# Gate and up tiles of a feed-forward by Strassen's seven products

## The chip, the cores and the metric

The kernel runs on one core of one Trainium2 chip. The metric is the device time of one execution in microseconds, the median of several runs. Five engines matter: TensorE (matrix products, in the profile PE, its weight loads PEld), VectorE (DVE), ScalarE (ACT), GpSimd (POOL) and SyncE (SP, which issues the transfers).

## The reference

A trunk of two layers for 128 prompt tokens and 512 latent tokens, 640 together, 1024 channels wide, all in float32. Each layer normalizes, projects, runs three mixers (a gated convolution, attention, a bidirectional state-space scan), merges them, and then adds a feed-forward:

```
h = rms_norm(x, norm2_g) * (1 + scale2) + shift2
x = x + gate2 * ((silu(h @ w_ffn_gate) * (h @ w_ffn_up)) @ w_ffn_down)
```

The gate and up matrices are 1024 x 2816 and the down matrix 2816 x 1024. shift2, scale2 and gate2 come from a modulation product of a condition vector with `w_ada`. The two groups of tokens share the weights and differ in the conditions.

## The kernel before

**Numbers.** A product of float32 is made of three products of float32r: each operand is split exactly into a high and a low part, and high x high, high x low and low x high are added up in PSUM. A product of 128 channels in, 128 channels out and 640 tokens is therefore three products times two halves of 320 tokens (HN), six matmuls of 128x128 weights against 320 columns (`gemm`, line 732). Activations are kept channels on partitions, as pairs of tiles (high, low) of 640 columns.

**Weights.** They come as a stream of blocks in the order of use (`order`, from line 283): a block of up to 1024 words per partition, 512 KB, is loaded by SyncE into one of three `wr` buffers (`w_load`, line 365). The `converter` (line 376) makes it a `wh` tile of a high part (a cast on ScalarE) and a low part (a subtraction on VectorE). There are three `wh` buffers (line 178), and a block may be converted when it is at most two ahead of the one that the products took last. `w_get` (line 393) hands a converted block to the products. Modulation blocks are in the same stream; they are used unsplit, in products of 32 condition rows (`ada_step`, line 545).

**Order of the work.** The order on each engine is fixed when the program is written out. The main products are a generator. Before each group of six matmuls it tells what they need, and `pump` (line 431) then emits those pieces of side work that can start earlier by a clock of estimated times. The converter is side work of the first priority. The estimates (`Clock`, `Engine`, from line 58) cost a matmul 133 ns for 320 columns, a VectorE instruction 70 ns and 1.04 ns a column, a ScalarE instruction 100 ns and 0.83 ns a column. Each engine then runs its list in order and waits on semaphores.

**The feed-forward** (line 1742 on) follows the second normalization (`norm`, line 660), which makes the eight pairs of h. It has two halves of 11 tiles of 128 hidden channels. For each tile the gate product (48 matmuls) and the up product (48) go to a PSUM tile each; `ev_g` makes tanh and a gated value, `ev_u` multiplies and splits the result into the hidden pair. After 11 tiles follow the eight tiles of the down product over those 11 blocks (66 matmuls each), added to x by `gated` (line 751), three VectorE instructions. In layer 0 one modulation block follows nearly each gate tile. The first pair of a feed-forward runs both tiles side by side (`pair_gemm`), since h is still being made.

After the second half's gate and up tiles of layer 0, `ssm_begin` starts the state-space side work of layer 1, which prepares its matrices under the second down product and the first stages of layer 1. The gate that reads its results (`glu`) comes after the query projections.

**Buffers.** PSUM has four tiles of two banks (`gps`). `c2` tiles of 640 columns: 57. `pt` tiles of 1280 columns (line 176): four, which attention uses, and the state-space side work; the feed-forward of before doesn't.

All instructions are recorded at one helper's line (L130), so the profile is read by tiles and shapes: `wh<-wr` is a conversion, `bps<-c,wh` a main product, `c<-bps` an evacuation, `bps<-wr,csT` a modulation product.

## Time and profile before

| | us |
|---|---|
| median of 3 runs | 2639.64 |
| lowest and highest | 2638.81, 2642.4 |
| span of the profiled execution | 2643.2 |
| TensorE busy | 2554.0 |
| VectorE busy | 1580.0 |
| ScalarE busy | 1016.2 |
| GpSimd busy | 0.2 |

The profiled execution has no other time of its own on record than its span, which is 3.6 us over the median of the runs and 0.8 over the highest. Busy times of matmuls overlap one another, so a busy TensorE says that it has no gap and not how quick it is; that is read from the number of matmuls in a stretch. A wait is put down to the instruction whose signal came last.

### The profile page before, as it was taken

How to read it: one execution, taken by the hardware profiler on the slowest of the kernel's cores; microseconds unless marked ns; L12 is line 12 of the kernel's file. 1: busy time of each engine (PE TensorE's matmuls, PEld its weight loads, DVE VectorE, ACT ScalarE, POOL GpSimd, SP SyncE). 2: the span in 40 equal slices, each digit the busy share in tenths (PEclk: the TensorE clock that was granted, in tenths of full speed). 3: DMA queues.
4: the chain of work that ended last, by engine and by line, in shares of the span. 5: the costliest groups of instructions: out<-in, count | busy, mean ns of one | idle time of the engine just before them, and what ended most of it. 6: DMA issues, size and time to landing. Idle time of an engine off the chain costs nothing. (4 is left out here: it accounts for less than half of the span.)

```text
span 2643.2 us, 44920 instructions
## 1 busy us (share of the span) xinstructions
PE 2554.0 (97%) x18683; PEld 2460.0 (93%) x18683; DVE 1580.0 (60%) x2982; ACT 1016.2 (38%) x1835; POOL 0.2 (0%) x4
## 2 busy tenths in 40 slices
PE   6999999999899999999989999999998999999998
PEld 4899999999888999999989999989998989999998
DVE  5888887788744433233677897578776453333333
ACT  4334336566622421122253333466664242212222
POOL 0000000000000000000000000000000000000000
PEclk8999999999999999999989999999999999999999
DMA  9433321121057233333334233212211633223222
GB/s 266 133 110 110 110 76 54 60 69 41 9 168 215 75 110 88 88 112 105 89 119 113 66 112 102 74 51 69 59 41 56 206 113 88 62 75 88 72 63 73
DMA packets 404411, 250.53 MB, mean 95 GB/s; under 512 B 57768, under 2 KB 392432, under 8 KB 404208
## 3 DMA queue, kind: packets, MB, share of 16 engines
q1 hardware_dynamic: 404208, 247.66, 31.9%
q8 instruction: 147, 2.41, 0.4%
q14 instruction: 56, 0.46, 0.1%
HBM read 227.49 MB, written 20.12 MB: 94 GB/s over the span
## 5 line engine op out<-in xcount | busy, mean ns | idle before, releaser
L130 PE MATMUL bps<-c,wh 128*128 128x320 f32 x12672 | 1952.1, 312 | 37.9 <-ACT c L130 18.4
L130 PEld LDWEIGHTS bps<-c,wh 128*128 128x128 f32 x12672 | 1876.4, 189 | 75.9 <-issue 25.1
L130 DVE TENSOR_TENSOR wh<-wr,wh 128x1024 fp32r<-128x1024 f32 (+2 forms) x308 | 353.8, 1153 | 223.6 <-ACT wh L130 213.8
L130 DVE TENSOR_TENSOR c<-c,c 128x512 f32<-128x512 f32 (+10 forms) x722 | 407.5, 590 | 71.6 <-ACT c L130 62.1
L130 ACT CAST wh<-wr 128x1024 fp32r<-128x1024 f32 (+2 forms) x308 | 303.7, 990 | 318.1 <-PE bps L130 177.9
L130 DVE SCALAR_TENSOR_TENSOR c<-c,bps 128x640 f32<-128x640 f32 (+1 forms) x108 | 83.2, 771 | 245.9 <-ACT c L130 169.6
L130 ACT CAST c<-c 128x640 fp32r<-128x640 f32 (+3 forms) x172 | 102.3, 621 | 327.0 <-DVE c L130 322.4
L130 DVE TENSOR_TENSOR c<-c,bps 128x640 f32<-128x640 f32 (+1 forms) x108 | 82.8, 769 | 205.9 <-PE bps L130 202.6
L130 PE MATMUL bps<-wh,c 128*128 128x256 f32 x1440 | 181.0, 284 | 2.0 <-ACT c L130 1.8
L130 ACT ACTIVATE c<-bps 128x640 f32<-128x640 f32 (+1 forms) x108 | 71.7, 664 | 285.3 <-PE bps L130 274.7
L130 PE MATMUL bps<-ident,c 128*128 128x128 f32 (+1 forms) x1115 | 159.1, 280 | 19.6 <-DVE c L130 7.4
L130 PEld LDWEIGHTS bps<-wh,c 128*128 128x128 f32 x1440 | 175.4, 191 | 2.7 <-ACT c L130 2.2
L130 PE MATMUL bps<-c,c 128*128 128x320 f32 (+2 forms) x960 | 159.5, 297 | 8.3 <-ACT c L130 4.5
L130 PEld LDWEIGHTS bps<-ident,c 128*128 128x128 f32 (+1 forms) x1115 | 132.6, 145 | 30.2 <-issue 8.9
L130 PEld LDWEIGHTS bps<-c,c 128*128 128x128 f32 x960 | 134.3, 191 | 13.4 <-ACT c L130 9.6
L130 ACT COPY c<-bps 64x256 f32<-64x256 f32 (+7 forms) x210 | 85.5, 445 | 155.8 <-PE bps L130 154.3
L130 ACT ACTIVATE c<-c 128x640 f32<-128x640 f32 (+4 forms) x93 | 65.3, 716 | 206.7 <-DVE c L130 206.5
L130 ACT ACTIVATE c<-bps,mx 128x640 f32<-128x640 f32 (+1 forms) x160 | 113.3, 713 | 36.1 <-DVE mx L130 35.6
L130 DVE TENSOR_REDUCE mx<-bps 128x1 f32<-128x640 f32 (+1 forms) x136 | 109.6, 809 | 26.4 <-PE bps L130 26.1
L130 DVE TENSOR_TENSOR pt<-bps,pt 128x640 fp32r<-128x640 f32 (+1 forms) x136 | 109.1, 810 | 15.3 <-ACT pt L130 14.5
L130 ACT CAST pt<-bps 128x640 fp32r<-128x640 f32 (+1 forms) x136 | 92.3, 687 | 26.6 <-PE bps L130 25.7
L130 PE MATMUL bps<-pt,c 128*128 128x256 f32 (+1 forms) x656 | 96.0, 292 | 2.9 <-DVE pt L130 2.1
(98 smaller groups left out, 1072.7 us busy)
## 6 DMA issues: line engine op xcount, KB each, us to landing
wr<-in_w_in_dram SPq DMA_DIRECT2D x104, 512.0 KB
wr<-in_w_ada_dram SPq DMA_DIRECT2D x62, 512.0 KB
wr<-in_w_ffn_gate_dram SPq DMA_DIRECT2D x44, 512.0 KB
wr<-in_w_ffn_up_dram SPq DMA_DIRECT2D x44, 512.0 KB
c<-in_w_ada_dram SPq DMA_DIRECT2D x68, 256.0 KB
wr<-in_w_ffn_down_dram SPq DMA_DIRECT2D x32, 384.0 KB
wr<-in_w_ffn_down_dram SPq DMA_DIRECT2D x32, 320.0 KB
wr<-in_w_proj_attn_dram SPq DMA_DIRECT2D x16, 512.0 KB
```

What stands on the lines that cost most here:

```text
L130: res = f(*args, **kw)
```

## The change

From the fourth tile of hidden channels on (PLAIN = 3), the gate tile and the up tile of the same 128 channels become one 2x2 product: the columns of the matrix on the left are gate and up, its rows the first and the last 512 input channels, and the right operand's columns are the two halves of 320 tokens. Of the eight products of quarters, 12 matmuls each (four blocks of channels, three float32r products), Strassen's scheme (in the form with shared sums) needs seven.

- **Sums of activations** (`sums`, once a layer, as side work): from the unsplit h, which `norm` now keeps (`plain`), four combinations of quarters for each of the four pairs of channel blocks, split again.
- **Sums of weights** (`pair_units`): a pair of tiles comes as two blocks, ra (upper rows of gate and up) and rb (lower rows). Three combinations on VectorE give four units: (ra, difference), (two sums), (rb plain), (one sum alone). The high and low parts of the first, second and fourth are made as before. For the third, ScalarE writes the high part of rb and, with scale -1, minus the high part (the write rounds to float32r), and a transfer issued by GpSimd with `accum_op=add` adds rb to the latter in place. `rb` and the sums live in `pt` tiles.
- **Products** (`glu_pair`): the seven quarter products go to the four banks of two PSUM tiles X and Y, with additions of first results in tiles z and e. `quarters` (not shown) cuts h and its sums into the right operands. The rest of the evacuation is side work (`tail`).
- **Four parts**: tiles 0 to 3, then 4 to 9, 10 to 15 and 16 to 21, each followed by its share of the down products (4 or 6 blocks). So x is added to four times.
- The normalization makes its channel blocks in the order KS = 0, 4, 1, 5, ..., and the first pair takes them in that order.
- In layer 0 the modulation blocks are put behind the pairs, as many as before.

The diff, cut to its core (in the rest comments are dropped and arguments passed on):

```diff
@@ -44,8 +44,9 @@
 WR = 3
 NTILES = 57
 RES = 1
-FF_HALF = KF // 2
-FD_ROWS = (((0, 6), (6, 5)), ((11, 6), (17, 5)))
+FF_PARTS = ((0, 4), (4, 6), (10, 6), (16, 6))
+PLAIN = 3
+KS = (0, 4, 1, 5, 2, 6, 3, 7)
 GQ = 4
 GE = GQ * NCH
...
+    def wpair(key, src1, src2, c0):
+        for h in range(2):
+            order.append((key + (h,), [src[512 * h:512 * h + 512, c0:c0 + 128] for src in (src1, src2)], 4, 128))
+        units.extend(key + (j,) for j in range(4))
...
         for m in range(8):
             tblk(("o", l, m), a["w_out"][l], 0, KD, 128 * m, 128)
         ada_gap(GN)
-        for half in range(2):
-            for m in range(FF_HALF * half, FF_HALF * half + FF_HALF):
-                tblk(("fg", l, m), a["w_ffn_gate"][l], 0, KD, 128 * m, 128)
-                tblk(("fu", l, m), a["w_ffn_up"][l], 0, KD, 128 * m, 128)
+        for r0, nr in FF_PARTS:
+            for m in range(r0, r0 + nr):
+                if m < PLAIN:
+                    tblk(("fg", l, m), a["w_ffn_gate"][l], 0, KD, 128 * m, 128)
+                    tblk(("fu", l, m), a["w_ffn_up"][l], 0, KD, 128 * m, 128)
+                else:
+                    wpair(("fgu", l, m), a["w_ffn_gate"][l], a["w_ffn_up"][l], 128 * m)
+                    ada_blk(ada_n(("fgu", l, m)))
             for m in range(KD):
-                for r0, nr in FD_ROWS[half]:
-                    wblk(("fd", l, m, r0), a["w_ffn_down"][l], r0, nr, 128 * m, 128)
+                wblk(("fd", l, m, r0), a["w_ffn_down"][l], r0, nr, 128 * m, 128)
         ada_gap(GF)
     assert not ada_o
...
-        key, src, nr, ncol = order[i]
-        t = wrp.tile([128, 1024], F32, tag="wr", name="wr")
-        clk.ring("wr", t.name, WR)
-        sp.dma_start(t[:, :nr * ncol].rearrange("p (k m) -> p k m", k=nr), src.rearrange("(k p) m -> p k m", p=128))
+        key, srcs, nr, ncol = order[i]
+        if key[0] == "fgu" and key[3]:
+            t = f32(ptp.tile([128, 2, TK], F32R, tag="pt", name="pt").rearrange("p a b -> p (a b)"))
+        else:
+            t = wrp.tile([128, 1024], F32, tag="wr", name="wr")
+            clk.ring("wr", t.name, WR)
+        n = nr * ncol
+        for j, src in enumerate(srcs):
+            sp.dma_start(t[:, n * j:n * j + n].rearrange("p (k m) -> p k m", k=nr), src.rearrange("(k p) m -> p k m", p=128))
         wraw[i] = t
         wst["load"] += 1
...
     def converter():
-        for i, (key, src, nr, ncol) in enumerate(order):
-            yield lambda: i in wraw and i < wst["use"] + 2 - wst["pair"]
+        u = 0
+        pair = []
+        for i, (key, srcs, nr, ncol) in enumerate(order):
+            def may():
+                return i in wraw and u < wst["use"] + 2 - wst["pair"]
+            yield may
             if key[0] == "ada":
-                wtile[i] = wraw.pop(i)[:, :nr * ncol].rearrange("p (k m) -> p k m", k=nr)
+                wtile[u] = wraw.pop(i)[:, :nr * ncol].rearrange("p (k m) -> p k m", k=nr)
+                u += 1
+                continue
+            n = nr * ncol
+            if key[0] == "fgu":
+                pair.append(wraw.pop(i))
+                if key[3]:
+                    for hl in pair_units(pair, lambda: u < wst["use"] + 2 - wst["pair"]):
+                        if hl is None or callable(hl) or isinstance(hl, tuple):
+                            yield hl
+                            continue
+                        wtile[u] = hl[0]
+                        u += 1
+                    pair = []
                 continue
             yield wraw[i], "act", "wh"
             t = wraw.pop(i)
-            hl = whp.tile([128, 2, 1024], F32R, tag="wh", name="wh")
-            clk.ring("wh", hl.name, 3)
-            n = nr * ncol
+            hl = wh_tile()
             act.copy(hl[:, 0, :n], t[:, :n])
             yield hl, "dve"
             sub(hl[:, 1, :n], t[:, :n], f32(hl[:, 0, :n]))
-            wtile[i] = [hl[:, r, :n].rearrange("p (k m) -> p k m", k=nr) for r in range(2)]
+            wtile[u] = [hl[:, r, :n].rearrange("p (k m) -> p k m", k=nr) for r in range(2)]
+            u += 1
             w_load()
+    def pair_units(pair, may):
+        ra, rb = pair
+        q = lambda t, j: t[:, 512 * j:512 * j + 512]
+        def unit(hl, n):
+            return [[hl[:, r, :n].rearrange("p (j k m) -> p j k m", k=4, m=128) for r in range(2)]]
+        def both(t, n):
+            hl = wh_tile()
+            act.copy(hl[:, 0, :n], t[:, :n])
+            yield hl, "dve"
+            sub(hl[:, 1, :n], t[:, :n], f32(hl[:, 0, :n]))
+            yield unit(hl, n)
+        yield ra, rb, "dve"
+        sm_ = f32(ptp.tile([128, 2, TK], F32R, tag="pt", name="pt").rearrange("p a b -> p (a b)"))
+        stt(q(sm_, 0), q(ra, 1), -1.0, q(rb, 1), OP.mult, OP.subtract)
+        sub(q(ra, 1), q(ra, 0), q(ra, 1))
+        yield ra, "act", "wh"
+        yield from both(ra, 1024)
+        yield may
+        yield sm_, "dve"
+        stt(q(sm_, 1), q(sm_, 0), -1.0, q(ra, 0), OP.mult, OP.subtract)
+        w_load()
+        yield sm_, "act", "wh"
+        yield from both(sm_, 1024)
+        yield may
+        yield rb, "act", "wh"
+        hl = wh_tile()
+        act.copy(hl[:, 0], rb[:, :1024])
+        act.activation(hl[:, 1], rb[:, :1024], AF.Copy, scale=-1.0)
+        pool.dma_start(f32(hl[:, 1]), rb[:, :1024], accum_op=OP.add)
+        yield unit(hl, 1024)
+        yield may
+        yield rb, sm_, "dve"
+        sub(q(sm_, 0), q(rb, 0), q(sm_, 1))
+        w_load()
+        yield sm_, "act", "wh"
+        yield from both(sm_, 512)
...
+    def quarter(ps, b, w, i, xs, first):
+        K = len(xs)
+        for k, x in enumerate(xs):
+            yield (w[0],) + x + (() if k else (ps,))
+            for n, (r, s) in enumerate(((0, 0), (0, 1), (1, 0))):
+                mm(ps[:, b, 0:HN], w[r][:, i, k, :], x[s], first and k == 0 and n == 0, k == K - 1 and n == 2)
+    def sums(ts_, hs, out):
+        pend = []
+        for j in range(4):
+            a, b = v2(ts_[j]), v2(ts_[j + 4])
+            yield ts_[j], ts_[j + 4], "dve"
+            t1, t2 = c2(), c2()
+            sub(t1[:, 0:HN], a[:, 0], a[:, 1])
+            sub(t1[:, HN:], b[:, 1], a[:, 1])
+            add(t2[:, 0:HN], b[:, 1], t1[:, 0:HN])
+            sub(t2[:, HN:], b[:, 0], t2[:, 0:HN])
+            ts_[j] = ts_[j + 4] = None
+            r = []
+            for t in (t1, t2):
+                hi, lo = c2(F32R), c2(F32R)
+                act.copy(hi, t)
+                yield hi, "dve"
+                sub(lo, t, f32(hi))
+                r.append((hi, lo))
+            out.append(r)
...
+    def glu_pair(l, m, x, hid):
+        X, Y = gps(), gps()
+        z = c2()
+        w = w_get(("fgu", l, m, 0))
+        yield from quarter(X, 0, w, 0, x["b11"], True)
+        act.copy(z[:, 0:HN], X[:, 0, 0:HN])
+        yield from quarter(Y, 1, w, 1, x["t3"], True)
+        act.copy(z[:, HN:], Y[:, 1, 0:HN])
+        w = w_get(("fgu", l, m, 1))
+        yield from quarter(Y, 0, w, 0, x["t1"], True)
+        add(z[:, HN:], z[:, HN:], Y[:, 0, 0:HN])
+        yield from quarter(X, 1, w, 1, x["t2"], True)
+        w_ahead(2)
+        e = f32(ptp.tile([128, 2, TK], F32R, tag="pt", name="pt").rearrange("p a b -> p (a b)"))
+        add(z[:, 0:HN], z[:, 0:HN], X[:, 1, 0:HN])
+        add(e[:, 2 * HN:3 * HN], z[:, 0:HN], z[:, HN:])
+        w = w_get(("fgu", l, m, 2))
+        yield from quarter(X, 0, w, 0, x["b21"], False)
+        s = c2()
+        act.activation(s[:, 0:HN], X[:, 0, 0:HN], AF.Tanh, scale=0.5)
+        stt(s[:, 0:HN], s[:, 0:HN], 1.0, X[:, 0, 0:HN], OP.add, OP.mult)
+        release(X)
+        yield from quarter(Y, 1, w, 1, x["t4"], False)
+        w = w_get(("fgu", l, m, 3))
+        yield from quarter(Y, 0, w, 0, x["b22"], False)
+        add(v2(e[:, 0:TK]), pv2(Y), z[:, None, 0:HN].to_broadcast([128, 2, HN]))
+        release(Y)
+        act.activation(s[:, HN:], e[:, 0:HN], AF.Tanh, scale=0.5)
+        def tail():
+            yield s, "dve"
+            stt(s[:, HN:], s[:, HN:], 1.0, e[:, 0:HN], OP.add, OP.mult)
+            mul(s, s, e[:, HN:3 * HN])
+            hi, lo = c2(F32R), c2(F32R)
+            act.copy(hi, s)
+            yield hi, "dve"
+            sub(lo, s, f32(hi))
+            hid.append((hi, lo))
+        side = Side(tail(), -0.4)
+        for _ in range(ada_n(("fgu", l, m))):
+            yield from ada_step()
+        return side
...
             if m == 6:
                 ada_flush()
         stat.append(pend.pop(0))
-        hs = yield from norm(stat, xs, s2T[l], modT[l][:, 3], FILL2)
+        hp = [None] * KD
+        hs = yield from norm(stat, xs, s2T[l], modT[l][:, 3], FILL2, KS, hp)
+        tt_ = []
+        side = Side(sums(hp, hs, tt_), -0.3)
         ssm = None
-        for half in range(2):
+        for part, (m0, nm) in enumerate(FF_PARTS):
             hid = []
-            for m in range(FF_HALF * half, FF_HALF * half + FF_HALF):
+            tails = []
+            for m in range(m0, m0 + nm):
+                if m >= PLAIN:
+                    if not side.done:
+                        pump(until=side)
+                    tails.append((yield from glu_pair(l, m, quarters(hs, tt_), hid)))
+                    continue
                 s = c2()
                 def ev_g(ps):
@@ -1755,23 +1937,26 @@
                     hid.append(split(s))
                 if m == 0:
-                    yield from pair_gemm(("fg", l, m), ("fu", l, m), hs, ev_g, ev_u)
+                    yield from pair_gemm(("fg", l, m), ("fu", l, m), hs, ev_g, ev_u, KS)
                     continue
                 yield from tile_gemm(("fg", l, m), hs, ev_g)
                 yield from tile_gemm(("fu", l, m), hs, ev_u)
-            if not half:
+            for x in tails:
+                if not x.done:
+                    pump(until=x)
+            final = m0 + nm == KF
+            if not final:
                 ada_flush(l, 5)
             else:
                 ada_flush()
                 stat = []
+                hs = tt_ = None
                 ssm = ssm_begin(l + 1) if l + 1 < DEPTH else None
             for m in range(KD):
                 ps = gps()
-                for r0, nr in FD_ROWS[half]:
-                    w = w_get(("fd", l, m, r0))
-                    r1 = r0 - FF_HALF * half
-                    yield from gemm(ps, w, 0, hid[r1:r1 + nr], r1 == 0, r1 + nr == FF_HALF)
-                if half:
+                w = w_get(("fd", l, m, m0))
+                yield from gemm(ps, w, 0, hid)
+                if final:
                     clk.calm = m >= KD - 2 and l + 1 < DEPTH
                     if l + 1 < DEPTH and m >= 8 - GF:
```

## Rows read from the trace of the kernel before

**Rows 1.** The page: busy times of the engines, and TensorE's granted clock in 40 slices

```profile
PE 2554.0 (97%) x18683; PEld 2460.0 (93%) x18683; DVE 1580.0 (60%) x2982; ACT 1016.2 (38%) x1835; POOL 0.2 (0%) x4
...
PEclk8999999999999999999989999999999999999999
```

**Rows 2.** Stretches: length, then busy PE, PEld, DVE, ACT, POOL; clock; DMA share; GB/s

```profile
860.84:902.50 41.66, 41.66 (x282) 40.33 (x283) 21.91 (x25) 20.22 (x30) 0.00 (x0) 1.00 0.25 74
1024.00:1101.50 77.50, 77.50 (x531) 77.50 (x530) 22.59 (x38) 13.68 (x17) 0.00 (x0) 1.00 0.27 79
1276.90:1354.50 77.60, 72.01 (x523) 70.15 (x521) 69.63 (x212) 23.96 (x48) 0.00 (x0) 1.00 0.32 85
...
2380.00:2540.00 160.00, 160.00 (x1093) 160.00 (x1092) 55.49 (x60) 36.85 (x44) 0.00 (x0) 1.00 0.26 75
```

**Rows 3.** Timeline of weight loads (layer 0) and evacuations (layer 1): start, length, instructions

```profile
1001.44 0.16 PEld L130 LDWEIGHTS bps<-wr,csT 128*32 128x32 f32 x8 [0.19 <-issue]
1002.01 14.08 PEld L130 LDWEIGHTS bps<-c,wh 128*128 128x128 f32 x96 [0.41 <-issue]
1016.28 0.16 PEld L130 LDWEIGHTS bps<-wr,csT 128*32 128x32 f32 x8 [0.19 <-issue]
...
2182.82 0.70 ACT L130 ACTIVATE c<-bps 128x640 f32<-128x640 f32 x1 [2.77 <-PE bps L130]
...
2196.90 0.70 ACT L130 ACTIVATE c<-bps 128x640 f32<-128x640 f32 x1 [4.50 <-PE bps L130]
```

**Rows 4.** Timeline of VectorE in the first down product of layer 0

```profile
1053.23 1.13 DVE L130 SCALAR_TENSOR_TENSOR c<-bps,g2T,c 128x128 f32<-128x128 f32 x3 [2.82 <-PE bps L130]
...
1062.91 1.14 DVE L130 SCALAR_TENSOR_TENSOR c<-bps,g2T,c 128x128 f32<-128x128 f32 x3 [2.82 <-PE bps L130]
```

**Rows 5.** Groups by shape, VectorE, then ScalarE: count, busy us, mean ns, idle before

```profile
L130 DVE TENSOR_TENSOR wh<-wr,wh 128x1024 fp32r<-128x1024 f32 x244 | 297.5, 1222 | 141.0 <-ACT wh L130 131.3
L130 DVE TENSOR_TENSOR c<-c,c 128x640 fp32r<-128x640 f32 x116 | 93.2, 824 | 58.4 <-ACT c L130 58.3
L130 DVE TENSOR_TENSOR c<-c,c 128x512 f32<-128x512 f32 x136 | 91.7, 688 | 2.9
L130 DVE TENSOR_TENSOR c<-c,bps 128x640 f32<-128x640 f32 x92 | 75.0, 819 | 203.1 <-PE bps L130 202.6
L130 DVE TENSOR_TENSOR c<-c,bps 128x320 f32<-128x320 f32 x16 | 7.7, 482 | 2.8 <-ACT c L130 2.8
...
L130 ACT CAST wh<-wr 128x1024 fp32r<-128x1024 f32 x244 | 254.5, 1046 | 196.0 <-DMA wr<-in_w_proj_attn_dram 78.8 <-PE bps L130 77.0 <-DMA wr<-in_w_out_dram 32.5
L130 ACT CAST c<-c 128x640 fp32r<-128x640 f32 x116 | 81.8, 727 | 327.0 <-DVE c L130 322.4 <-issue 3.6
L130 ACT CAST c<-bps 128x512 fp32r<-128x512 f32 x32 | 19.0, 594 | 0.0
L130 ACT ACTIVATE c<-c 128x320 f32<-128x320 f32 x16 | 7.6, 474 | 15.7 <-DVE c L130 15.7
L130 ACT ACTIVATE c<-bps 128x320 f32<-128x320 f32 x16 | 7.0, 436 | 23.0 <-PE bps L130 15.7 <-issue 7.3
```

**Rows 6.** Timeline: issues of weight loads by SyncE, and the casts that waited for them

```profile
2101.62 0.37 SPq L130 DMA_DIRECT2D wr<-in_w_out_dram  x1
...
2107.82 0.37 SPq L130 DMA_DIRECT2D wr<-in_w_out_dram  x1
...
2105.49 1.05 ACT L130 CAST wh<-wr 128x1024 fp32r<-128x1024 f32 x1 [2.54 <-DMA wr<-in_w_out_dram]
...
2112.85 1.05 ACT L130 CAST wh<-wr 128x1024 fp32r<-128x1024 f32 x1 [2.11 <-DMA wr<-in_w_out_dram]
```

**Rows 7.** DMA queues, 1359.5 to 1366 (the spill): packets, MB, share of 16 engines

```profile
q1 hardware_dynamic: 989, 2.11, 86.3%
```

**Rows 8.** DMA queues, 2380 to 2530 (layer 1's feed-forward, weight loads)

```profile
q1 hardware_dynamic: 22728, 11.45, 26.1%
```

**Rows 9.** Timeline of SyncE: the last store of state-space outputs, and their gate's weights

```profile
1657.45 0.34 SPq L130 DMA_DIRECT2D yd<-c  x1
...
1694.76 12.77 SPq L130 DMA_DIRECT2D wr<-in_w_glu_dram  x2
```

More of the change, by code (lines that the diff above doesn't have):

```diff
@@ L389, in converter, with w_ahead @@
             sub(hl[:, 1, :n], t[:, :n], f32(hl[:, 0, :n]))
[L390 removed]
+            wtile[u] = [hl[:, r, :n].rearrange("p (k m) -> p k m", k=nr) for r in range(2)]
+            u += 1
             w_load()
+    def pair_units(pair, may):
[34 more added lines that the diff above has]
+        yield from both(sm_, 512)
     def w_get(key):
[L394 to L395 removed]
+        u = wst["use"]
+        assert units[u] == key, (units[u], key)
         wst["use"] += 1
[L397 removed]
+        while u not in wtile:
             cvt.step()
[L399 removed]
+        return wtile.pop(u)
+    def w_ahead(n):
+        while wst["use"] + n - 1 not in wtile and wst["use"] + n - 1 < len(units):
+            cvt.step()
     sides = []
@@ L664, in norm @@
         clk.calm = False
-        hs = []
+        hs = [None] * KD
         def low(k):
@@ L669, in low @@
             sub(lo, h, f32(hi))
-        ts_ = []
-        for k in range(KD):
+            if plain is None:
+                ts_[k] = None
+        ts_ = [None] * KD if plain is None else plain
+        last = None
+        for n, k in enumerate(ks):
             yield ps, "dve"
             t = c2()
-            ts_.append(t)
+            ts_[k] = t
             mul(v2(t), v2(xs[k]), pv2(ps))
-            if k == KD - 1:
+            if n == KD - 1:
                 release(ps)
-            if k:
-                low(k - 1)
-            hs.append((c2(F32R), c2(F32R)))
+            if n:
+                low(last)
+            last = k
+            hs[k] = (c2(F32R), c2(F32R))
             act.activation(t[:, :TP], t[:, :TP], AF.Identity, bias=sh[:, k, 0:1], scale=sc[:, k, 0:1])
@@ L684, in norm @@
             act.copy(hs[k][0], t)
-        low(KD - 1)
+        low(last)
         return hs
@@ L729, in reload_x, with gemm @@
         return xs
-    def gemm(ps, w, c0, acts, first=True, last=True):
+    def gemm(ps, w, c0, acts, first=True, last=True, ks=None):
         K = len(acts)
-        for k in range(K):
+        for i, k in enumerate(ks or range(K)):
             x = acts[k]
-            if last and k >= K - RES:
+            if last and i >= K - RES:
                 clk.spare = 1
-            yield (w[0],) + x + (() if k else (ps,))
+            yield (w[0],) + x + (() if i else (ps,))
             for n, (r, s) in enumerate(((0, 0), (0, 1), (1, 0))):
```

31 lines of the change are left out of this document (20 added, 11 removed).

## Prediction

> **What bounds the kernel now.** The page's busy times come first [rows 1]: TensorE is busy 97% of the span, VectorE 60%, ScalarE 38%, GpSimd not at all, and TensorE's granted clock stands at the upper level, 2.4 GHz, but for dips. Then a table of stretches [rows 2]: in the down products of layer 0 and in half of layer 1's feed-forward TensorE has no idle time (77.50 of 77.50 us, 160.00 of 160.00), with VectorE at a third. So the feed-forward costs what its matmuls cost. The last gives 160.00 / 1093 = 146 ns for one. The timeline gives it exactly [rows 3]: 96 weight loads, one for each matmul of a gate and an up tile, take 14.08 us, 146.7 ns each. A pair of tiles takes 14.08 us in layer 1 (two evacuations one after the other start at 2182.82 and 2196.90) and 14.84 in layer 0, where each is followed by one modulation block of 0.76 us. A down tile of 11 blocks, 66 matmuls, takes 9.68 us [rows 4], the same rate.
>
> **What goes.** 19 of the 22 pairs of each layer need 7 x 4 x 3 = 84 matmuls instead of 96. 19 x 12 x 0.1467 = 33.4 us per layer, 66.9 in all, if TensorE stays without waits; a pair then takes 12.32 us (13.08 with its modulation block). The down products keep their number.
>
> **What TensorE has to wait for now.** A pair takes four units of converted weights, of 24, 24, 24 and 12 matmuls: 3.52, 3.52, 3.52 and 1.76 us; they start at 0, 3.52, 7.04 and 10.56. There are three wh buffers, so the third unit (rb, the plain quarters) gets the buffer of the fourth unit of the pair before, free at 0, and must be there at 7.04. What stands between:
>
> 1. VectorE adds 640 columns from PSUM, 0.82, and ScalarE takes the tanh of 320, 0.47 [rows 5]; both are issued ahead of the unit's casts and ScalarE runs in order.
> 2. ScalarE casts 1024 columns, 1.05, and copies them negated (no row has this; the cast's 1.05). With steps of about 0.06 between engines that is 3.4 us after the last matmul.
> 3. In layer 1 the copy of the first product stands in front too: by the planner's costs the tanh ends 1.30 us after the pair, and the last point of the first quarter at which side work is emitted is at 1.20 (9 matmuls of 133 ns). That product is done at 1.76, its copy takes 0.44 to 0.47, so the casts end at 4.3. In layer 0 the modulation block puts the planner's TensorE 1.1 us later, and the casts go first.
> 4. GpSimd's accumulating transfer, 512 KB. Call it L, from the end of the negated copy to its landing.
>
> Behind it lie units three and four, 5.28 us. So a pair takes 3.4 + L + 5.28 = 8.7 + L in layer 0 (the modulation block lies inside), 9.6 + L in layer 1, and no less than 13.08 and 12.32.
>
> **What L is.** The trace has no transfer issued by GpSimd, and none that adds. A plain load of 512 KB lands 3.87 and 5.03 us after its issue (2101.62 to 2105.49, 2107.82 to 2112.85), the second behind modulation loads [rows 6]. Loads in 512-byte packets move 11.45 MB in 26.1% of 16 engines' 150 us, 18.3 GB/s for an engine, 293 for all [rows 8]: 1.79 us for a block, which leaves 2.1 us fixed. Long rows (the residual's spill, 2560 bytes each) move 2.11 MB in 86.3% of 6.5 us, 376 GB/s [rows 7]: 1.4 us for one pass over 512 KB. An accumulation has to read both operands. If the reads overlap fully, L is 2.1 + 1.4 = 3.5; if they follow one another, 4.9; with three passes behind a whole weight block 2.1 + 4.2 + 1.8 = 8.1. Below, no issue can be cheaper than a load's without its fixed part: 1.4. I take 4.2, between one pass and two; the nearest row is the 3.87 of the load.
>
> A rule of the Trainium skill bears on this, "DMA: Bandwidth & Descriptors", the section on the anatomy of one DMA on the gpsimd path: about 2.0 us fixed and the bytes over 436 GB/s, that is 3.2 us for this size, by which the sum below would end at 2599. It is stated for plain copies; our load's 2.1 fixed agrees, its rate doesn't (293 GB/s). No run here shows a GpSimd transfer yet.
>
> With 4.2, layer 0 needs 12.9 and stays at 13.08: 19 x 1.76 = 33.4 us gained. Layer 1 takes 13.8: 19 x 0.28 = 5.3 us gained. Together 38.7 of the 66.9.
>
> **VectorE and ScalarE in a pair** [rows 5]. VectorE: four combinations of 512 columns (4 x 0.69), low parts of 1024, 1024 and 512 (2.44 + 0.69), five instructions on 320 (5 x 0.48), three on 640 (3 x 0.82): 10.8 us, where it had 4.9. It fits in 12.3 with little to spare. ScalarE: four of 1024 columns, 0.6, four of 320 and one of 640, 7.3 us. The order matters more: the e tile comes from a ring of four which it shares with rb and sm, and takes the place of rb. So the add into e waits on VectorE until the transfer has landed, and behind it stand two combinations (1.38), then the cast (1.05) and the low part (1.22) of the next pair's first unit, with a 0.48 between: e 0.48 and these give 4.6 plus some 0.3 of steps, 4.9 us after the landing, against TensorE's 5.28. It holds by 0.4 us.
>
> **Smaller terms.**
> - Ends of parts, four in a layer instead of two. From the last matmul to the last hidden half: 0.82 + 0.47 + 0.48 + 0.82 + 0.73 + 0.82 and steps, 4.4 us; the first down tile's other blocks cover 5 x 0.88 = 4.4 (parts of six) or 2.6 (part of four), and down weights' low parts (0.95) run on VectorE between. Before, 10 blocks covered 2.4 us of it. I take 4 a layer, 8 together; bounds 0 and 16.
> - Starts of parts, three a layer: combinations, cast and low part 3.7 us, with the gated sums (1.30) between 4.9, against a last down tile of 5.28 or 3.52: 3 together, bounds 0 and 8.
> - The sums of activations: 16 halves at 0.48 and 8 low parts at 0.82, 14.3 us of VectorE. The three plain pairs have 41.66 - 21.91 = 19.8 us free [rows 2]. I take 1; if the first paired tile needs that time as well, up to 5.
> - The second down stretch of layer 0 covers the state-space preparation of layer 1. It was 8 x 9.68 = 77 us and becomes 8 x 5.28 = 42. VectorE did 69.63 us there against 22.59 in a down stretch without it [rows 2], so 47 us of side work, 21 of which now come later. Its last output was stored at 1657.45 and the gate that reads it had its weights issued at 1694.76 [rows 9]: 37 us of slack. I take 5; bounds 0 and 21.
> - Twice as many gated sums (1.30 us on VectorE for each of 16 more tiles a layer) lie under down products in which VectorE is 29% busy: nothing. Where VectorE is full they cost up to 21 us a layer. Gate and up blocks come as two transfers of 256 KB instead of one of 512: an issue takes 0.37 us [rows 6], SyncE is free most of the time: nothing.
>
> 17 us together. Sum: -38.7 + 17 = -21.7, and 2643.2 - 21.7 = 2621.5 by the profiled execution's span. The median of the runs, 2639.64, lies 3.6 below that span, so the forecast is 2618.
>
> **Rivals.**
> - **All hidden.** L is 2.7 or less, or the planner puts the casts first in layer 1 also and L is small. All 66.9 are gained, less 17: 2590. For it: GpSimd is idle and long rows are quick. Against: 2.7 is less than any load's landing in this trace.
> - **The transfer ends the pair, later than two passes.** This is the other side. At L above 4.4 each further us costs 38 us over both layers, and the sum changes sign at 19 x (8.7 + L - 14.84) + 19 x (9.6 + L - 14.08) + 17 = 0, L = 4.86. At 6 the pairs take 14.7 and 15.6: -2.7 + 28.9 + 17 = +43, 2683; at 8.1 it would be +123. For it: two passes alone give 4.9, weight loads run on the same engines a quarter of the time, and the second load above needed 5.03. Against: the fixed part may be smaller without HBM.
> - **GpSimd can't write descriptors while VectorE works.** The transfer's start waits for the instruction on VectorE, up to 1.22 us here [rows 5]: L 5.4, pairs of 14.1 and 15.0, +20, 2660. The Trainium skill has this against the change, "SBUF — State Buffer", the section on who interferes with whom: copies in two-port modes lock GpSimd out, a tensor_tensor with both inputs in SBUF holds only the read side. VectorE's work in a pair is of the second kind, so by that rule it would mostly not come; no row of before shows it either way.
> - **VectorE's order sets the pair.** One more low part (1.22) between the add into e and the next first unit, and 4.9 becomes 6.1, 0.8 over TensorE's 5.28: 38 x 0.8 = 30 us, -21.7 + 30 = +9, 2648. For it: the margin of 0.4 us and VectorE at 10.8 of 12.3. Against: the low part of the second unit is allowed only after the fourth unit is taken.
>
> **Chances.** The forecast 0.38 (with L from 3.5 to 4.6 it alone spans 2605 to 2630); all hidden 0.15; a late transfer 0.24; descriptors 0.08; VectorE's order 0.15. Bounds of L and of the smaller terms and the rivals' times give 2586 to 2690 for eight in ten. 0.2% is 5 us, about what can be told from no change. Faster: forecast and all hidden, and a little of VectorE's order, 0.55. Same: 0.09, from the cases around the sign change. Slower: 0.36.
>
> **What would show it.** Right: 38 transfers from GpSimd, 456 matmuls fewer, pairs of about 13.1 us in layer 0 and 13.8 in layer 1, TensorE's waits inside pairs at the third unit, ended by that transfer, about 4.2 us from the negated copy's end; VectorE near 10.8 us a pair; the state-space branch done before its gate. Wrong: waits at the first unit of pairs, ended by VectorE's low part (its order), gaps above 2 us at the third unit (a late transfer), pairs of 12.3 with no wait (all hidden), or a wait at layer 1's state-space gate.

## The result, and the profile after

The changed kernel takes 2787.7 us (median of 4 runs, 2785.9 to 2799.2) against 2641.0 before (4 runs), a ratio of 1.0562 [1.0539, 1.0586]. The forecast was 2618, in a range of 2586 to 2690: wrong in sign. The profiled execution's span is 2785.4 us, 142.2 above that of before.

The page of the changed kernel, busy times; it answers to [rows 1].

```profile
PE 2557.8 (92%) x18235; PEld 2425.5 (87%) x18235; DVE 1849.5 (66%) x3507; ACT 1160.6 (42%) x2079; POOL 33.0 (1%) x42
```

448 matmuls fewer are recorded, near the 456 that were to go, yet TensorE's busy time has not fallen and its share has: TensorE waits. Two stretches of paired tiles (length, busy times of the engines, clock, DMA share, GB/s), layer 0 and layer 1, against no idle time in the plain pairs and in half of layer 1's feed-forward of before [rows 2]:

```profile
1109.00:1206.00 97.00, 78.38 (x485) 68.93 (x484) 52.09 (x76) 34.73 (x54) 5.05 (x6) 0.96 0.39 101
2488.00:2592.00 104.00, 84.93 (x543) 79.31 (x542) 62.50 (x91) 40.78 (x61) 5.16 (x6) 1.00 0.36 87
```

Every pair issues one accumulating transfer, so the timeline of GpSimd (start, length) gives the pair's period as [rows 3] gave it before:

```profile
1109.30 0.86 POOL L131 DMA_DIRECT2D wh<-pt  x1 [54.38 <-ACT wh L131]
...
1205.26 0.86 POOL L131 DMA_DIRECT2D wh<-pt  x1 [17.37 <-ACT wh L131]
...
2524.12 0.86 POOL L131 DMA_DIRECT2D wh<-pt  x1 [16.08 <-DVE pt L131]
2541.05 0.86 POOL L131 DMA_DIRECT2D wh<-pt  x1 [16.07 <-DVE pt L131]
```

Layer 1: 16.94 us a pair here, where 14.08 were. Layer 0: five periods from 1109.30 to 1205.26, 19.19 on average, where 14.84 were. Of the 19 pairs of a layer 15 follow another pair of the same part. By the issue times those 15 periods add up to 294.3 us in layer 0 and 262.0 in layer 1 (17.5 on average), 72 and 51 us more than at the periods of before: 122 of the 142 us. The first pair of a part isn't longer: from one part's last transfer to the next part's first (1054.05 to 1109.30) it is 55.25 us, and eight down tiles of 5.28 leave 13.0 of that.

The group view of the transfers' target says how long a transfer takes from issue to landing, most of L, the number on which the prediction had turned:

```profile
L131 POOL DMA_DIRECT2D wh<-pt x38: 859/859/1002, 912.9 to 2717.1; - x38
...
DMA to landing us min/median/max: 4.5/4.5/5.1
```

The prediction counts L from the end of the negated copy, and the issue comes 0.3 us behind that (the copy ends at 2540.76, the issue is at 2541.05). So L is 4.8 us where 4.2 was forecast. (In layer 1 the profile puts the end of GpSimd's wait down to an instruction of VectorE. In layer 0, where it names ScalarE, the issue is 0.3 us behind the copy too.) What was late was above all the issue. The timeline of TensorE in one pair of layer 1 (it begins at 2533.92, 3.52 us before the first wait below), with what ended each wait:

```profile
2538.90 0.56 PE L131 MATMUL bps<-c,wh 128*128 128x320 f32 x2 [1.46 <-ACT wh L131]
2540.16 3.49 PE L131 MATMUL bps<-c,wh 128*128 128x320 f32 x22 [0.70 <-DVE wh L131]
2544.33 0.53 PE L131 MATMUL bps<-c,wh 128*128 128x320 f32 x2 [0.67 <-DVE c L131]
2545.62 5.54 PE L131 MATMUL bps<-c,wh 128*128 128x320 f32 x36 [0.77 <-DMA wh<-pt]
```

and of ScalarE in the same pair:

```profile
2534.82 0.47 ACT L131 ACTIVATE c<-pt 128x320 f32<-128x320 f32 x1 [3.01 <-DVE pt L131]
2535.72 0.43 ACT L131 COPY c<-bps 128x320 f32<-128x320 f32 x1 [0.43 <-PE bps L131]
2536.71 0.73 ACT L131 CAST c<-c 128x640 fp32r<-128x640 f32 x1 [0.56 <-DVE c L131]
2537.48 0.42 ACT L131 COPY c<-bps 128x320 f32<-128x320 f32 x1
2537.80 1.99 ACT L131 CAST wh<-pt 128x1024 fp32r<-128x1024 f32 x2
2539.70 1.06 ACT L131 ACTIVATE wh<-pt 128x1024 fp32r<-128x1024 f32 x1
```

ScalarE is idle for 3 us, waiting for the sum behind the pair's last matmul, then takes the tanh, both copies of products and the tail's cast. Only then come the casts of the second and third unit (the two of 1.99 us) and the negated copy. The second copy waits for a product that TensorE ends 3.52 us into the pair, and the negated copy ends at 6.84. TensorE wanted the second unit at 2537.44; its high half is there at 2538.85. The transfer is issued at 2541.05, 7.13 us into the pair. 7.13 + 4.5 + 5.28 (units three and four) = 16.9: the period. Over the pairs from 2488 to 2592 TensorE's waits are these (us in total, times, longest):

```profile
PE bps L131 <- ACT wh L131: 7.3, 5, 1.5
PE bps L131 <- DVE c L131: 3.9, 6, 0.7
PE bps L131 <- DMA wh<-pt: 3.8, 5, 0.8
PE bps L131 <- DVE wh L131: 3.5, 5, 0.7
```

So the transfer ends the last wait of the pair, and the second unit's cast and low part (7.3 and 3.5) cost TensorE more than it does (3.8).

In layer 0 it is VectorE too. TensorE, VectorE, then ScalarE and GpSimd, around the start of a pair:

```profile
1152.03 6.79 PE L131 MATMUL bps<-c,wh 128*128 128x320 f32 x34 [1.08 <-DMA wh<-pt]
...
1160.86 3.49 PE L131 MATMUL bps<-c,wh 128*128 128x320 f32 x22 [0.99 <-DVE wh L131]
```

```profile
1158.85 0.82 DVE L131 TENSOR_TENSOR pt<-bps,c 128x640 f32<-128x640 f32 x1 [1.83 <-PE bps L131]
1159.59 1.22 DVE L131 TENSOR_TENSOR wh<-wr,wh 128x1024 fp32r<-128x1024 f32 x1
```

```profile
1164.60 0.43 ACT L131 COPY c<-bps 128x320 f32<-128x320 f32 x1
...
1164.91 1.06 ACT L131 CAST wh<-pt 128x1024 fp32r<-128x1024 f32 x1
...
1165.86 1.06 ACT L131 ACTIVATE wh<-pt 128x1024 fp32r<-128x1024 f32 x1
...
1167.22 0.86 POOL L131 DMA_DIRECT2D wh<-pt  x1 [18.89 <-ACT wh L131]
```

VectorE is idle until the pair before ends, for its sum of 640, and the low part of the next first unit, whose cast had ended at 1158.15, stands behind that sum. The third unit's casts stand behind the copy of the second product, which TensorE ends at 1164.35. The negated copy ends at 1166.92, 8.2 us after the pair before ended at 1158.74, and the transfer is issued at 8.5; with 4.5 and 5.28 that is 18.3.

The first of TensorE's rows shows one thing more: 34 matmuls take 6.79 us, where the same 34 take 5.25 in run 6 below. A window over it has a granted clock of 0.88, so a part of it ran at the lower level (1.2 GHz, the upper one being 2.4), after five waits in the pair. A later window of layer 0, 1184.80 to 1206.00, with such waits too, has 1.00, as layer 1's stretch above. Other pairs of layer 1 have it: 22 matmuls at 2363.59 take 5.03 us instead of 3.49. There the transfer has landed before TensorE wants it, and the pair takes 17.45.

```profile
1144.90:1158.80 13.90, 11.35 (x64) 10.40 (x68) 5.76 (x9) 4.27 (x7) 0.86 (x1) 0.88 0.31 76
```

### The profile page after: what moved, and what is told of

Read it like the earlier page. It is cut to its first block, busy times and chain, and to the rows that moved or that the text cites. A ratio compares the mean times of both kernels' runs of the same rounds, so it can differ in the third digit from the quotient of the medians.

```text
span 2785.4 us, 45262 instructions
## 1 busy us (share of the span) xinstructions
PE 2557.8 (92%) x18235; PEld 2425.5 (87%) x18235; DVE 1849.5 (66%) x3507; ACT 1160.6 (42%) x2079; POOL 33.0 (1%) x42
## 5 line engine op out<-in xcount | busy, mean ns | idle before, releaser
L131 PEld LDWEIGHTS bps<-c,wh 128*128 128x128 f32 x12216 | 1840.5, 192 | 236.0 <-DVE wh L131 61.0
L131 DVE TENSOR_TENSOR c<-c,c 128x512 f32<-128x512 f32 (+11 forms) x762 | 430.8, 592 | 56.7 <-ACT c L131 45.8
L131 ACT CAST wh<-wr 128x1024 fp32r<-128x1024 f32 (+2 forms) x270 | 264.5, 982 | 363.6 <-PE bps L131 159.6
L131 DVE TENSOR_TENSOR wh<-wr,wh 128x1024 fp32r<-128x1024 f32 (+2 forms) x270 | 306.9, 1141 | 149.7 <-ACT wh L131 148.9
L131 ACT COPY c<-bps 128x320 f32<-128x320 f32 (+8 forms) x287 | 118.5, 440 | 173.3 <-PE bps L131 171.3
L131 DVE SCALAR_TENSOR_TENSOR c<-c,bps 128x320 f32<-128x320 f32 (+1 forms) x108 | 70.5, 653 | 179.7 <-ACT c L131 102.9
L131 ACT CAST c<-c 128x640 fp32r<-128x640 f32 (+3 forms) x188 | 113.7, 628 | 132.4 <-DVE c L131 123.7
L131 DVE TENSOR_TENSOR c<-c,bps 128x320 f32<-128x320 f32 (+1 forms) x146 | 88.5, 609 | 84.7 <-PE bps L131 80.2
L131 DVE SCALAR_TENSOR_TENSOR c<-bps,g2T,c 128x128 f32<-128x128 f32 (+2 forms) x192 | 72.6, 434 | 106.9 <-PE bps L131 106.7
L131 ACT CAST wh<-pt 128x1024 fp32r<-128x1024 f32 (+1 forms) x114 | 101.5, 906 | 35.9 <-DVE pt L131 26.2
```

Of the source, the lines that this page charges most:

```text
L131: res = f(*args, **kw)
```

## The experiments

Theory A: the loss is the order in which work stands in ScalarE's and VectorE's queues, with the waits that PSUM tiles add. Its rivals: the transfer, VectorE's amount of work, four parts instead of two, the planner's prices.

**1. Four parts alone.**

```
-PLAIN = 3
+PLAIN = KF          (and no sums of activations)
```

> All 22 pairs of each layer plain (96 matmuls), the feed-forward still in four parts; no sums of activations, no transfer. Theory A (the 147 us are lost inside the paired tiles, by the order of work on ScalarE and VectorE): 2640 to 2650, since nothing of the pairs is left. Theory B (ends and starts of parts and the lost cover for the state-space work cost what the prediction booked): 2641 + 16 = 2657. Theory C (the parts are what costs): over 2680.

2654.2 us, 1.0039 [1.0026, 1.0052]. Theory C falls; 10 us are between A and B. Where they lie is seen by the norms' first sums, which mark the ends of layer 0's feed-forward and the start of layer 1's. Before, then four parts:

```profile
1354.54 1.25 PE L130 MATMUL bps<-ones,c 128*128 128x1 f32 x10
...
2148.52 1.17 PE L130 MATMUL bps<-ones,c 128*128 128x1 f32 x10
```

```profile
1352.19 1.26 PE L131 MATMUL bps<-ones,c 128*128 128x1 f32 x10 [1.15 <-DVE c L131]
...
2159.24 1.17 PE L131 MATMUL bps<-ones,c 128*128 128x1 f32 x10
```

794.0 and 807.1 us: 13 us are lost in the stretch between, in which VectorE is busy 589 us instead of 561: the state-space work that has lost its cover comes there. That this work is the cause was not tested by itself. The feed-forward itself is not longer (2.0 us less in layer 0, 0.3 more in layer 1). By the same marks the changed kernel's feed-forwards are 78 us longer than before in layer 0 and 54 in layer 1, and the stretch between them 14.

**2. The transfer left out.**

```
-        pool.dma_start(f32(hl[:, 1]), rb[:, :1024], accum_op=OP.add)
```

> The accumulating transfer of the third unit is left out, so its low half holds the negated high half and the sum is wrong by it; every other instruction stays. Theory A: only the waits ended by the transfer go, 19 x (1.08 + 0.75) = 35 us by the changed kernel's rows and a little for restarts: 2745 to 2755, and the other waits (ScalarE's cast and VectorE's low part of the second unit, the two PSUM tiles) stay or grow. Theory of the prediction's second rival (the transfer ends the pair): pairs fall to their matmuls, 19 x (19.0 - 13.1) + 19 x (16.9 - 13.0) = 186 us less, under 2620.

2751.9, 1.0407 [1.0389, 1.0424]: 36 us, the sum that A expected, but not where it expected it. The two feed-forwards (length, busy times, clock, DMA share, GB/s), in the changed kernel, then without the transfer:

```profile
845.14:1428.93 583.79, 503.78 (x3258) 462.72 (x3257) 325.28 (x586) 192.46 (x283) 16.48 (x19) 0.96 0.38 100
2236.90:2785.00 548.10, 479.70 (x3098) 459.01 (x3096) 312.89 (x506) 199.75 (x287) 16.33 (x19) 0.96 0.32 83
```

```profile
847.16:1396.83 549.67, 484.77 (x3259) 447.80 (x3257) 325.23 (x586) 192.53 (x283) 0.00 (x0) 0.99 0.31 88
2203.91:2750.00 546.09, 481.98 (x3098) 463.54 (x3096) 312.60 (x506) 199.67 (x287) 0.00 (x0) 0.95 0.23 66
```

Layer 0 is 34 us shorter, layer 1 only 2. The transfer had ended 16.6 us of TensorE's waits in layer 0 and 5.3 in layer 1. The other waits are as they were, within 0.5 us by kind (apart from one new wait of 2.1); what is left goes with the clock, which rises in layer 0 and falls in layer 1. There a pair takes 15.92 us where the clock stays up and 17.45 where it doesn't. So the transfer alone does not set the pair.

**3. The second unit's products swapped**, so that neither meets a read of its tile's other bank that isn't done.

```
-        yield from quarter(Y, 0, w, 0, x["t1"], True)
-        add(z[:, HN:], z[:, HN:], Y[:, 0, 0:HN])
         yield from quarter(X, 1, w, 1, x["t2"], True)
+        add(z[:, 0:HN], z[:, 0:HN], X[:, 1, 0:HN])
+        yield from quarter(Y, 0, w, 0, x["t1"], True)
...
-        add(z[:, 0:HN], z[:, 0:HN], X[:, 1, 0:HN])
+        add(z[:, HN:], z[:, HN:], Y[:, 0, 0:HN])
```

> Second unit's two products in the other order: the one into X first, then the one into Y. Theory A: the waits for VectorE's and ScalarE's reads of the other bank of the same PSUM tile go (layer 0 0.73 + 0.67, layer 1 0.67 per pair): 19 x (1.40 + 0.67) = 39 us, 2745 to 2750; a few us more where fewer gaps mean fewer stretches at half clock. Rival (the pair is set by a later wait, the cast or the transfer, and these waits only hide it): 2780 to 2790, the idle time coming back at the third unit.

2781.0, 1.0524 [1.0506, 1.0541]. The rival was right: the PSUM waits went and most of the time came back (8.6 us in four waits for the transfer between 1101 and 1194 in layer 0; in the changed kernel 4.3 in four between 1109 and 1206).

**4. The second unit's cast first.**

```
         w = w_get(("fgu", l, m, 0))
+        w_ahead(1)
```

> The second unit's cast and low part are always issued ahead of the copies of the pair's first two products. Theory A: layer 1 loses the waits for that cast and low part, 1.46 + 0.71 and a restart of 0.25, 19 x 2.4 = 46 us; layer 0 0.38 x 19 = 7: 2735. Rival (one queue for another: the cast stands before the copies, the products that need Y's other bank free wait longer, and VectorE's low part holds up the add of the pair before): within 15 us of 2788 either way.

2733.5, 1.0340 [1.0325, 1.0356], as A expected in the sum. Its split is another: the feed-forward is 22 us shorter in layer 0 and 32 in layer 1, where 7 and 46 were expected. Layer 1 falls to 14.8 us a pair. What is left in layer 0 are mainly these waits of TensorE between 1101 and 1194 (us in total, times, longest):

```profile
PE bps L131 <- ACT c L131: 8.2, 5, 1.9
PE bps L131 <- DVE wh L131: 5.0, 5, 1.0
```

The cast now stands before the copies, and the product into Y waits up to 1.9 us for the copy out of Y's other bank.

**5. Both small edits together**, the diffs of 3 and 4.

> The planner's order with both small edits: the second unit's cast and low part ahead of the copies, and the second unit's product into X before the one into Y. Theory A (the swap gave little because the second unit's cast was late anyway; with that gone it pays): the waits for PSUM tiles of the run with the cast first, 1.6 + 0.6 in layer 0 and 1.2 + 0.6 in layer 1, go: 2733 - 19 x 4.0 = 2657, range 2645 to 2690 since the next wait (the transfer, the low parts) may show. Rival (only an order written out for all of the pair helps): over 2710.

2745.5, 1.0397 [1.0381, 1.0412]: a miss for A, slower than the cast alone, as the rival had it. Layer 0's feed-forward gains 18 us on the cast alone, layer 1's loses 30. The waits in layer 1 between 2440 and 2540 say why:

```profile
PE bps L131 <- DMA wh<-pt: 11.1, 5, 4.2
PE bps L131 <- DVE wh L131: 3.6, 5, 1.6
```

The PSUM waits are gone, and TensorE comes sooner to the third unit, whose casts stand behind the second unit's: the transfer is up to 4.2 us late. Single repairs of the queue hand the wait on.

**6. The whole order written out.** A pair's steps are emitted by hand, each engine's in this order:

```
ScalarE: u2 cast, u2 negated, tanh(previous), copy X, copy Y, u3 cast, tail cast(previous),
         next u0 cast, tanh X, next u1 cast
VectorE: combination for u3, tail(previous), u3 low, z += X, tail low(previous), combination A,
         z += Y, combination B, sum, combination C, next u0 low, silu X, next u1 low, add into e
TensorE: second unit into X, then into Y;     u0 to u3: the pair's four units
```

> The whole computation, with the order of a pair's work on ScalarE and VectorE written out: the third unit's cast, negated copy and transfer first on ScalarE in a pair, the second unit's cast and low part in the pair before, the tail of a pair in the next one, the second unit's products into X before Y. Theory A (order and PSUM tiles are the whole loss): all 67 us of matmuls saved, less the 10 that four parts cost: 2644 + 10 - 67 = 2587, with the sums of activations up to 2600; pairs of 12.3 to 12.6 and 13.1 to 13.3 us and no stretch at half clock in the pairs. Rival B (the transfer): issued 2.4 us into a pair and landing 4.5 us later it is 0.1 us early for the third unit in layer 1; 1 us late would be 19 us more, 2606 to 2620. Rival C (VectorE's 10.8 us in an order without slack): pairs of 13.5 or more in layer 1, 2620 to 2650.

2632.5, 0.9956 [0.9942, 0.9970]: 155 us less than the changed kernel with the same instructions in its pairs. TensorE in layer 1, then the issue of transfers:

```profile
2271.76 62.50 PE L131 MATMUL bps<-c,wh 128*128 128x320 f32 x425
```

```profile
2284.86 0.86 POOL L131 DMA_DIRECT2D wh<-pt  x1 [11.46 <-ACT wh L131]
2297.18 0.86 POOL L131 DMA_DIRECT2D wh<-pt  x1 [11.46 <-ACT wh L131]
```

Five pairs without a wait, 12.32 us each, the bare matmuls: the transfer of 4.5 us and VectorE's work fit. Layer 0 keeps 13.7 (five periods from 1084.16 to 1152.59) instead of 13.1, and the wait there is rival B's (1000 to 1190):

```profile
PE bps L131 <- DMA wh<-pt: 4.6, 5, 1.3
```

The transfers' landing in 1080 to 1200, where four of the six are issued 1.8 us behind the issue of a modulation block's load:

```profile
DMA to landing us min/median/max: 4.5/5.9/6.9
```

From 2270 to 2340, in layer 1, it is 4.5 in every one. The total is 45 us above A's 2587; 13 of them are this transfer (next run), the others are taken up below.

**7. The written order with VectorE's low half.**

```
-        act.activation(h2[:, 1], rb[:, :1024], AF.Copy, scale=-1.0)
-        pool.dma_start(f32(h2[:, 1]), rb[:, :1024], accum_op=OP.add)
+        sub(h2[:, 1], rb[:, :1024], f32(h2[:, 0]))
```

> As the run with the written order, with the third unit's low half as a VectorE subtraction of 1024 columns (1.22 us) instead of negated copy and transfer. VectorE then has 10.8 + 1.2 = 12.0 us a pair against 12.3 of matmuls in layer 1, 13.1 in layer 0. Theory A: VectorE becomes the bound in layer 1, pairs of 12.6 to 13.5, 5 to 20 us slower than the run with the transfer, 2595 to 2610. Rival B (the transfer is what is late): faster than the run with the transfer.

2619.4, 0.9911 [0.9896, 0.9926]: rival B was right, VectorE is no bound. A stretch of layer 0 and one of layer 1:

```profile
1100.00:1180.00 80.00, 80.00 (x562) 76.97 (x561) 55.13 (x84) 28.68 (x44) 0.00 (x0) 1.00 0.41 119
2370.00:2430.00 60.00, 60.00 (x411) 60.00 (x410) 51.87 (x77) 27.35 (x42) 0.00 (x0) 1.00 0.26 75
```

The pairs of these stretches run without idle time now, yet 32 us to 2587 are missing. By the marks of run 1, less 33.4 us a layer, some 25 of them lie in layer 0's feed-forward and 8 in layer 1's. TensorE's waits in layer 0's add up to 22.6 us, where run 1 has 4.5, and its clock is 0.97, where run 1 has 0.99. Most of the waits lie outside the paired tiles, such as these (the second plain pair of layer 0, its last down products, the second plain pair of layer 1):

```profile
878.84 23.13 PE L131 MATMUL bps<-c,wh 128*128 128x320 f32 x140 [4.44 <-DVE wh L131]
...
1312.92 28.13 PE L131 MATMUL bps<-c,wh 128*128 128x320 f32 x176 [3.30 <-DVE wh L131]
...
2179.61 44.99 PE L131 MATMUL bps<-c,wh 128*128 128x320 f32 x290 [3.86 <-DVE wh L131]
```

**8. The swap undone in the written order**, the diff of 3 backwards.

> The written order with the second unit's products back in their first order: into Y before X. Theory A (reads of one bank of a PSUM tile hold up products into its other bank): the product into Y's first bank waits for ScalarE's copy from its second bank, some 0.5 us, the third unit's first product for VectorE's sum from X's second bank, 0.67 as in the changed kernel: 38 x 1.1 = 42 us on 2632.5, 2665 to 2680, a part of it hidden in layer 0 where the transfer is late anyway. Rival (the waits only hide others, as with the swap in the planner's order, which gave 7 us): within 8 us of 2632.

2681.4, 1.0145 [1.0130, 1.0161], 49 us more: A, a little over its range. Waits between 2420 and 2520, in each of five pairs one of either kind, 13.95 us a pair:

```profile
PE bps L131 <- DVE c L131: 2.9, 5, 0.6
PE bps L131 <- ACT c L131: 2.6, 5, 0.5
```

What gave 7 us in the planner's order is worth 49 where little else is late.

**9. The second unit's cast late again**, and behind it the third unit's casts and transfer, as in the changed kernel; the rest as written (`adv` emits a pair's conversions up to the named one, `ahead` those of the next pair).

```
-        adv(l, m, "u1l")
-        adv(l, m, "u2")
         prev[0]()
...
         act.copy(z[:, HN:], Y[:, 1, 0:HN])
+        adv(l, m, "u2")
...
-        ahead("u1c")
-        ahead("u1l")
```

> The written order (with the swap and the tails as they are), but the second unit's cast and low part, and behind them the third unit's cast, negated copy and transfer, stand behind the copies of the pair's first two products, as the planner had them. Theory A (this one place in ScalarE's queue is the main loss): the second unit's high half ends 1.5 us after TensorE wants it, the low half 0.7 later, the transfer is issued at 7.1 us in the pair instead of 2.4 and lands 2 us late: pairs of 12.3 + 2.4 + 2.1 = 16.8 us in layer 1 and about 17.5 in layer 0, 2632 + 19 x 4.5 + 19 x 3.6 = 2786; range 2740 to 2790. Rival (PSUM waits, low parts behind the sum of Y and half clock are as much to blame): under 2700.

2805.2, 1.0624 [1.0604, 1.0644]. The rival falls. The two largest waits from 2500 to 2600 are those of the changed kernel to the digit (there 7.3 and 3.5 over five pairs), and the pair is 16.9 us again (2555.08 to 2572.04):

```profile
PE bps L131 <- ACT wh L131: 7.3, 5, 1.5
PE bps L131 <- DVE wh L131: 3.5, 5, 0.7
```

That it is over the expected 2790 lies at the starts of parts: from a part's last transfer to the next part's first 59.0 us (1057.22 to 1116.23), where the changed kernel has 55.3. All six starts together are 26 us longer than there, while the 30 periods in the parts are 17 shorter. At a part's start the changed kernel still has the third unit's casts in front of both copies (the cast starts at 1106.99, the first copy at 1108.91). Here they stand behind them there too (1113.93, the second copy at 1113.61). The run moves the second and the third unit together; what each is worth by itself was not tested.

**10. True prices in the planner.**

```
-                    cost = max(n, 256) / 2.4
+                    cost = (n + 32) / 2.4
...
-                    clock.w[x], clock.by[x] = e + 2000, "dma"
+                    clock.w[x], clock.by[x] = e + (3500 if key == "pool" else 2000), "dma"
```

> The changed kernel with two prices of the planner set to what the trace shows: a matmul 146.7 ns instead of 133, GpSimd's transfer 4.5 us from issue to landing instead of 3. Theory A1 (the wrong prices make the planner's order): the casts come ahead of the copies by themselves, 2690 to 2740. Theory A2 (the order of emission, not the prices: a copy of a product is emitted when its quarter's last matmul is, whatever it costs): 2770 to 2800.

2834.0, 1.0727 [1.0709, 1.0745], worse than both and outside both ranges. Layer 0's pairs stay at 19.2 us; the first transfer of all starts at 938.8 instead of 912.9, so 26 us are lost ahead of any pair. The prices don't make the order in the pairs, as A2 had it. Why the rest of the kernel is ordered worse with them stays open.

**11 and 12. The best version**, run 7 with `PLAIN = 4`, and the same with the first edit of run 10.

> The written order with VectorE's low half in place of the transfer, and four plain pairs a layer instead of three, so that the sums of activations end before the first pair that reads them. Gained: the wait of 4.44 and 1.24 us at the first pair of layer 0, 3.86 of layer 1. Lost: 12 matmuls, 1.76 us a layer. 2619.4 - 9.5 + 3.5 = 2613. Rival (these waits come back in the first down products): 2619 to 2624.

> The best version with the planner's matmul at the 146.7 ns of the trace instead of 133. It touches the work outside the pairs alone: the last down products of layer 0, where casts stand behind state-space preparation for 12 us, and the whole middle of the kernel. Theory A (the price makes the planner push side work ahead of casts there): 2600 to 2610. Rival (the prices of the other engines were set against 133, as the run with two prices showed by 26 us lost ahead of the first pair): 2625 to 2660.

2616.8, 0.9901 [0.9886, 0.9916]: faster than both kernels, but only 2.6 us below run 7 where 6 were expected, and the intervals of the two ratios overlap. The trace says why. Of the waits that were to go only the 1.24 us have gone. The long one of layer 0 is still there, and layer 1's with 4.39:

```profile
877.77 23.25 PE L131 MATMUL bps<-c,wh 128*128 128x320 f32 x140 [4.44 <-DVE wh L131]
```

It lies in the second plain pair, so one more plain pair behind it can't take it away. With the true price 2653.4, 1.0047 [1.0030, 1.0064]: the rival. Layer 0's feed-forward begins 25 us later with that price (870.85 instead of 845.53), as in run 10.

## Why the prediction was wrong

- **The failed step** is the third item of "what TensorE has to wait for", the time at which the third unit's casts end. It put tanh, at most one copy and the two casts in front of the transfer: 4.3 us into the pair in layer 1, 3.4 in layer 0. The traces show 6.8 and 8.2 in the pairs that follow another pair. It left out that the casts stand behind the copy of the second product and behind the second unit's cast in the same queue. The second unit itself it took to be there in time, a wait put at nothing; in layer 1 TensorE waits 2.2 us a pair for its cast and low part. The casts' delay, 15 x 2.5 + 15 x 4.8 = 110 us, stands against 164 between the forecast's -22 and the measured +142. Run 9 puts this place back into an order that otherwise runs at the bare matmuls in layer 1 (run 6), and gets the changed kernel's pair and waits there. The tail's cast, which stands in front too, is not what counts: run 9 has it behind, with the same 16.9 us.
- **The form of the sum was right** for the pairs at the upper clock: casts' end + L + 5.28 gives 16.9 and 18.3 with the measured terms. But it is not the only chain of that length: without the transfer layer 1 gains 2 us in all (run 2). In pairs of 19.8 us in layer 0 the lower clock adds some 1.5 us and in those of 17.45 in layer 1 some 0.5, a term that the prediction did not have.
- **L was too small**: 4.8 by the prediction's own definition, where it took 4.2. By its own terms that is 19 x (0.4 + 0.6) = 19 us, which would have left the forecast of 22 us faster near no change, just short of the rival's sign change at 4.86. It does not make the loss of 142. The rival of a late transfer at 6 or 8.1 is rejected by the landing times, and as the main cause by run 2.
- **The Trainium skill's rule for transfers.** The 3.2 us that the prediction estimated from the Trainium skill ("DMA: Bandwidth & Descriptors", anatomy of one DMA on the gpsimd path) isn't met by this accumulating transfer: 4.5 from issue to landing.
- **Descriptors held up by VectorE**: not seen. From issue to landing it is 4.5 us at the median and 5.1 at most with VectorE busy 60% of layer 1's stretch, as the rule of the Trainium skill ("SBUF — State Buffer", who interferes with whom) had it for instructions with both inputs in SBUF.
- **VectorE**: the amount fits (runs 6 and 7, with 1.2 us more). Its order did cost, but elsewhere than the rival put it: the first unit's low part stands behind the sum that waits for the pair's last matmul, 0.99 us a pair in layer 0. The prediction's sign for it, a wait at the first unit ended by VectorE's low part, is there.
- **A wait that was not thought of**: in this program products into one bank of a PSUM tile wait for reads of the other. In the changed kernel it is 0.67 us a pair (VectorE's read) and in layer 0 0.73 more (ScalarE's), in run 8 49 us in all.
- **Smaller terms**, 17 forecast. By run 1 the parts cost 10 with the state-space cover at 13 (5 taken, bounds 0 and 21) and ends and starts at about -1 (11 taken). The sums of activations most likely make the waits of 4.4 and 3.9 us in the layers' second plain pairs in run 7 (1 taken, up to 5): run 1, which has no such sums, has no wait there.
- **"All hidden", 2590**, is what the arithmetic allows, but this order could not reach it. With the pairs' waits gone it is still 27 us away. The waits seen there are for casts and low parts in the second plain pairs and in layer 0's last down products; which of them can be moved wasn't tried, but for run 11.

## What to carry to other kernels

When TensorE's work is cut, write out each in-order engine's queue for one period and look for an instruction that waits for TensorE in front of one that TensorE will wait for; the shares of busy time (ScalarE 42%, VectorE 66%) don't show it. A single repair of such a queue may give nothing, or even lose, because the next wait runs under the first: the swap was worth 7, then 49 us, depending on what else was late. A prefetch must be issued early enough for its whole latency: a transfer of 4.5 us cost nothing issued at 2.4 us in a pair (run 6, layer 1), and issued at 7.1 it was what TensorE waited for last.

## What the runs showed of the hardware

- An accumulating transfer of 512 KB inside SBUF, issued by GpSimd, takes 0.86 us of GpSimd, is issued 0.3 us after the copy that it waits for, and lands 4.5 us after its issue. In layer 0 of run 6, where a modulation block's load is issued 1.8 us before most of them, it is 5.9 at the median and up to 6.9; that the load delays it was not tested by itself.
- TensorE's clock was granted below its upper level in some pairs of layer 0 with five short waits, of 0.4 to 1.1 us each, and not in others as broken: 34 matmuls 6.79 us instead of 5.25. It can eat what a removed wait gives: without the transfer layer 1's pairs take 15.92 us at the upper level and 17.45 with a stretch at the lower one (run 2). In run 6's and 7's stretches without waits it stays at 1.00.
